# Moving tile pools of a hybrid attention/recurrence block: head weights beside the recurrence, and three staging tiles for w_out

## The chip, the cores and the metric

The kernel runs on one core of a Trainium2 chip. The metric is the device time of one execution in microseconds (us); before the change its median was 1280.75 over 3 runs (1280.01 to 1283.48). The engines are TensorE (PE: matmuls; PEld: its weight loads), VectorE (DVE), ScalarE (ACT), GpSimd (POOL) and SyncE (SP), which issues nearly all DMAs here, in order, from one queue.

## The reference

One layer works on 2048 latent tokens (a grid of 32 rows and 64 columns) and 256 context tokens of width 1024:

```python
h  = rms_norm(x, g) * (1 + scale) + shift          # hc likewise from ctx
q, k, v, z_a, u, z_l = split(h @ w_in)             # w_in: 1024 x 3072, six parts of 512
k_c, v_c, u_c = parts of hc @ w_in
attn = neighbourhood_attention(rope(norm(q)), norm(q), rope(norm(k)), v, norm(k_c), v_c, rpb)
uc, ucc = depthwise_conv(u), depthwise_conv(u_c)   # width 4
y = forward RG-LRU(ucc, uc) + backward RG-LRU(ucc, uc)
mix = concat([attn * silu(z_a), y * silu(z_l)]) @ w_out
out = x + gate * mix
```

The attention has 8 heads of 64 channels, the recurrence 8 blocks of 64. A recurrence step is `h = a*h + b`, with `a` and `b` made from two sigmoid gates of `u` through block weights `lru_wa`, `lru_wx` of 64 x 64, one set for each direction. `gate` comes from the conditioning vector through `w_mod`.

## The kernel before

**Number format.** A product of full precision is made of three fast ones: every operand is split into a high part and the remainder (`hh`, `hl` for the tokens, `wh`, `wl` for weights; all float16 in the projections, a rounded 32-bit format in the recurrence and the output). So a group of weights goes through `wload` (DMA into `wraw`), and `wsplit` (L315): DVE reduces the greatest magnitude (L319), `allmax` and `pow2` make a power of two of it (two tiny matmuls in a PSUM bank `mm`, and some small DVE operations), ACT makes `wh` (L324), DVE `wl` (L325).

**Phase 1** (`phase1`, L483). `mods` forms the conditioning vectors from `w_mod`, `prep` the normalised and transposed tokens (`hh`, `hl`: 64 KB per partition, kept on the right side of SBUF), `tables` writes bias tables to DRAM. Then, for four groups c of 128 recurrence channels: `u_proj(c)` projects and convolves `u` into a tile `uc` (pool `uc`, two tiles), through staging tiles `us`; `lru(c)` (L411) makes the gates' matmuls for both directions (weights `gw`, split into `gh` and `gl`), and per direction exponentials, square roots and scans of 2304 columns on DVE. The sums of both directions are made by POOL (L471) and stored as `d_y` (L472). Inside `lru(c)`, a function `fill(d)` emits the projection of two blocks of the attention's gate `z_a` of group c (`silu_z`, tile `sz`), and in its first call asks for the next group of these weights (`z_group`). `gate` (L575) makes the output's gate from more `w_mod` rows; its tiles are in a pool of its own on the right.

**Phase 2** (`phase2`, L920). For each of eight heads, `head_proj` makes q, k, v (192 columns, L602 to L604) and `attention` the banded softmax and its product. The recurrence's gate `z_l` is made in between (`lru_gate`). The second half of `w_out` (k = 4 to 7) is split in phase 2 (L1020, on DVE).

**Output** (`build`, L1085). The pools `out` and `ow` open when phase 2's right pools have closed. The gate row is spread over the partitions (`grow`, L1096), the first half of `w_out` (k = 0 to 3) is loaded into one staging tile `wo` (L1012), copied to its high part on ACT (L1015) and subtracted on POOL (L1016), beside the attention of head 7. `out_half` loads a tile of the mix (`m`, L1028, two buffers) and splits it into `mh` (ACT, L1030) and `ml` (DVE, L1031); `out_sum` (L1034) multiplies; the result times `grow` is added to a tile `xo` of `x` and stored.

**What sets the order.** The code is written against a tile framework which plans each engine's order of instructions itself, by the dependencies and the order in which the program emits them. A tile of a tag gets its buffer in program order: the next tile of a tag with n buffers waits for the one n places before it. The PSUM banks (`mm`, `sl`, `pt` two each, `sc`, `po` one) are such tags too. A pool that is opened on the bytes of pools that have closed is planned behind the last instruction of those; at run time each tile waits for the users of its own bytes. `issue_after` and `later` shift an emission in the plan.

**Places in SBUF.** On the right lie, from the outer edge inward, `h` (64 KB), `z` (two tiles of 2 KB: `us`, `sz`, and in phase 2 `ry`), `w2` (head weights: `wraw` 6 KB, two pairs `wh`, `wl` of 3 KB), `w3` (6 KB) and `stg` (18 KB: `ST0`, `ST1`, `STc` and others). On the left lie the constants, `hc`, `w1` (weights of the u and z_a groups: two raw tiles, three pairs `wh`, `wl`; 20 KB), `uc` (18 KB), then `p0` until the preparation is over and after it `lru` (78 KB: `A`, `X`, `I` twice each, `uh`, `ul`, `gh`, `gl`, `gw`). `lru` reaches into the bytes which `w2` and the gate's tiles have from the right, so `w2` is opened behind `lru` (L573), and its `wraw` lies on `ul`. In phase 2, `att`, `w3` and `stg` lie on bytes of `lru`, `uc` and `w1` as well. In the output, `ow` (`grow`, `wo`, two `m`) lies inward of `out`, on `ST0`, `ST1` and `STc`.

Of the kernel before, what the change touches and what calls it, by code (L numbers as in the profile page):

```python
# [45 lines left out]
BW = [384, 512, 384]  # L46

MA = 6
HLV = (3, 7)

MX = 400
# [7 lines left out]
class K:  # L59
# [232 lines left out]
    def w_tiles(self, tag, n):  # L292

        if tag == "z":
            return [self.wp["z"].tile([128, KC, 128], F16, tag=x, name=x, bufs=3) for x in ("wh", "wl")]
        if tag == "l":
            return [self.wp["l"].tile([128, KC, 128], F16, tag=x, name=x, bufs=1) for x in ("wh", "wl")]
        return [self.wp["h"].tile([128, KC, 192], F16, tag=x, name=x, bufs=2)[:, :, 0:n] for x in ("wh", "wl")]

    def wload(self, parts, tag):  # L300

        n = sum(w for _, w in parts)
        wp = self.wp["z" if tag == "z" else "h"]
        if tag == "z":
            raw = wp.tile([128, KC, n], F32, tag="raw", name="wraw", bufs=2)
        else:
            raw = wp.tile([128, KC, 192], F32, tag="raw", name="wraw", bufs=1)[:, :, 0:n]
        wv = self.a["w_in"].rearrange("(k p) n -> p k n", p=128)
        o = 0
        for c, w in parts:  # L310
            self.nc.sync.dma_start(raw[:, :, o:o + w], wv[:, :, c:c + w])
            o += w
        return raw, n, tag
# [97 lines left out]
    def lru(self, c, uc, p, fill):  # L411
# [4 lines left out]
        t = lambda x: p.tile([128, N], F32, tag=x, name=x, bufs=2)  # L416
        A, X = t("A"), t("X")
        gl = p.tile([128, 4, 128], F32R, tag="gl", name="gl", bufs=1)
        gw = p.tile([128, 4, 128], F32, tag="gw", name="gw", bufs=1)
        nc.gpsimd.memset(gw, 0.0)  # L420
        for g, nm in enumerate(("lru_wa", "lru_wx")):
            for f in range(2):
# [60 lines left out]
    def phase1(self, left, right):  # L483
# [14 lines left out]
        with ExitStack() as s1:  # L498
# [20 lines left out]
                return uc  # L519

            with ExitStack() as s0:
                p0 = self.pool(s0, "p0")
                mods = self.mods(p0)
                next(mods)
                with self.tc.issue_after(self.last.ins):
                    g0 = self.wgroup([(CU, 128)], "z", early=True)
                xs = next(mods)
                with self.tc.issue_after(self.last.ins):
                    self.prep(p0, 2, 1, hhc, hlc, xs, True)
                    ug[0] = u_group(0, g0)  # L530
                    ug[1] = u_group(1)
                    nxt = self.prep_in(p0, a["x"], 4, 0)
                    for tb in range(4):
                        xs = nxt
                        if tb < 3:
                            nxt = self.prep_in(p0, a["x"], 4, tb + 1)
                        self.prep(p0, 4, 0, self.hh[tb], self.hl[tb], xs)
                    with ExitStack() as s3:
                        self.tables(self.pool(s3, "tab", side="right"))
                    self.softplus(p0)  # L540
                    ucs = [u_proj(0), u_proj(1)]
                    with ExitStack() as s3, self.tc.issue_after(self.xld.ins), self.tc.issue_after(self.hh_op.ins):
                        self.gate(self.pool(s3, "gate", side="right"))
            za = []

            def z_group():
                c = len(za)
                g = self.wgroup([(CZA + 128 * c, 128)], "z", slow=c > 0)
                nc.vector.tensor_scalar(self.zs[:, c:c + 1], g[2], 0.5, None, ALU.mult)
                za.append(g)  # L550
            with ExitStack() as s2:
                p = self.pool(s2, "lru")
                ug[2] = u_group(2)
                z_group()

                def z_units(c, d):
                    wh, wl, _ = za[c]
                    for tb in (2 * d, 2 * d + 1):
                        z = self.silu_z(self.zp, self.bank("mm"), wh, wl, self.zs[:, c:c + 1], tb)
                        dz = self.d_z[c][tb].rearrange("p (j f x) -> p f j x", j=4, f=2)  # L560
                        for f in range(2):
                            zf = z[:, 256 * f:256 * f + 256]
                            nc.sync.dma_start(dz[:, f, 0:3], zf[:, 32:224].rearrange("p (j x) -> p j x", j=3))
                            nc.sync.dma_start(dz[:, f, 3].rearrange("p (e x) -> p e x", e=2),
                                              bass.AP(zf.tensor, zf.offset, [list(zf.ap[0]), [224, 2], [1, 32]]))
                    if d == 0 and c < 3:
                        z_group()

                for c in range(4):
                    self.lru(c, ucs[c], p, lambda d, c=c: z_units(c, d))  # L570
                    if c < 2:
                        ucs.append(u_proj(c + 2))
            self.wp["h"] = self.pool(self.wright, "w2", bufs=2, side="right")  # L573

    def gate(self, p):  # L575

# [429 lines left out]
    def out_weights(self, ks, room):  # L1006

        nc = self.nc
        wo = self.a["w_out"].rearrange("(k p) n -> k p n", p=128)
        for k in ks:  # L1010
            w = room()
            nc.sync.dma_start(w, wo[k])  # L1012
            W = self.hp.tile([128, 2, D], F32R, tag="h", name="W")
            if k < 4:
                nc.scalar.copy(W[:, 0], w)  # L1015
                nc.gpsimd.tensor_tensor(W[:, 1], w, W[:, 0].bitcast(F32), ALU.subtract)  # L1016
            else:
                s = self.zs[:, k:k + 1]
                nc.scalar.activation(W[:, 0], w, AF.Copy, scale=s)
                nc.vector.scalar_tensor_tensor(W[:, 1], w, s, W[:, 0].bitcast(F32), ALU.mult, ALU.subtract)  # L1020
            self.wo.append((k, W))
# [34 lines left out]
    def out_proj(self, p, q, tb, opened):  # L1056
        nc, a = self.nc, self.a
        for i in range(4 * tb, 4 * tb + 4):
            pos = opened.pop(i, None)
            M1 = self.out_half(p, q, i, 1) if pos is None else None  # L1060
            M = self.out_half(p, q, i, 0)
            x = p.tile([128, D], F32, tag="xo", name="xo", bufs=2)
            for r, src in self.tile_rows(a["x"], i):
                nc.sync.dma_start(x[r], src)
            for f in range(2):
# [19 lines left out]
def build(tc, a):  # L1085
    with ExitStack() as ctx:
        k = K(ctx, tc, a)
        k.setup()
        k.vectors()
        with ExitStack() as right, ExitStack() as left:  # L1090
            k.phase1(left, right)
            att = k.phase2(left, right)
            p = k.pool(right, "out", side="right")
            q = k.pool(right, "ow", side="right")
            k.grow = q.tile([128, D], F32, name="grow")
            tc.nc.sync.dma_start(k.grow, bass.AP(k.d_g.tensor, 0, [[0, 128], [1, D]]))  # L1096
            k.out_weights(range(4), lambda: q.tile([128, D], F32, tag="wg", name="wo", bufs=1))
            op = k.out_open(p, q, 0)
            next(op)
            next(att)  # L1100
            with k.later(100):
                opened = {0: next(op)}
            for tb in range(4):
                next(att, None)
                k.out_proj(p, q, tb, opened)
# [34 lines left out]
```

## Time and profile before

| | us |
|---|---|
| median of 3 runs | 1280.75 (1280.01 to 1283.48) |
| the profiled execution | 1277.88 |
| its span in the profile | 1276.1 |
| PE busy | 1122.0 |
| DVE busy | 926.6 |
| ACT busy | 615.2 |
| POOL busy | 478.7 |

The span runs from the first to the last profiled instruction; the execution's own time is 1.78 us longer. The mean granted TensorE clock of this execution is 0.936 of full speed. Busy shares are averages over stages with different limits; the timelines of the places that the change touches say more.

### The profile page before, as it was taken

How to read it: one execution, taken by the hardware profiler on the slowest of the kernel's cores; microseconds unless marked ns; L12 is line 12 of the kernel's file. 1: busy time of each engine (PE TensorE's matmuls, PEld its weight loads, DVE VectorE, ACT ScalarE, POOL GpSimd, SP SyncE). 2: the span in 40 equal slices, each digit the busy share in tenths (PEclk: the TensorE clock that was granted, in tenths of full speed). 3: DMA queues.
4: the chain of work that ended last, by engine and by line, in shares of the span. 5: the costliest groups of instructions: out<-in, count | busy, mean ns of one | idle time of the engine just before them, and what ended most of it. 6: DMA issues, size and time to landing. Idle time of an engine off the chain costs nothing. (4 is left out here: it accounts for less than half of the span.)

```text
span 1276.1 us, 26205 instructions
## 1 busy us (share of the span) xinstructions
PE 1122.0 (88%) x9964; PEld 858.8 (67%) x9964; DVE 926.6 (73%) x2546; ACT 615.2 (48%) x1189; POOL 478.7 (38%) x863
## 2 busy tenths in 40 slices
PE   7777889689981879999999999999999976999997
PEld 1434345445540767889878898788887755778786
DVE  7798655989775677888978989798887863544432
ACT  1597116876773225555655555555556452231210
POOL 0144002234122087566566556565564552000000
PEclk9788899699996889999999999999999997999999
DMA  9846980011024414344543435334354346346452
GB/s 349 284 153 237 312 250 26 4 50 54 17 67 99 93 34 85 83 97 96 118 88 83 95 86 137 82 89 76 86 129 103 89 99 177 95 134 176 122 149 83
DMA packets 196014, 149.50 MB, mean 117 GB/s; under 512 B 129453, under 2 KB 168109, under 8 KB 195887
## 3 DMA queue, kind: packets, MB, share of 16 engines
q1 hardware_dynamic: 195887, 147.82, 43.3%
q8 instruction: 78, 1.28, 0.4%
q14 instruction: 49, 0.40, 0.1%
HBM read 96.42 MB, written 47.94 MB: 113 GB/s over the span
## 5 line engine op out<-in xcount | busy, mean ns | idle before, releaser
L602 PE MATMUL mm<-wh,hh 128*128 128x192 f16 x960 | 236.9, 247 | 0.0
L603 PE MATMUL mm<-wl,hh 128*128 128x192 f16 x960 | 236.9, 247 | 0.0
L604 PE MATMUL mm<-wh,hl 128*128 128x192 f16 x960 | 236.9, 247 | 0.0
L893 DVE TENSOR_TENSOR Pl<-pt,Ph 128x384 f16<-128x384 f32 (+1 forms) x256 | 127.4, 516 | 56.2 <-ACT Ph L892 55.7
L344 PE MATMUL mm<-hh,wh 128*128 128x512 f16 x384 | 150.3, 392 | 12.9 <-DVE sz L480 7.6
L345 PE MATMUL mm<-hl,wh 128*128 128x512 f16 x384 | 149.2, 389 | 8.3 <-POOL hl L289 7.9
L885 ACT ACTIVATE SP<-SP,nb 128x640 f32<-128x640 f32 (+1 forms) x128 | 110.7, 881 | 91.9 <-DVE nb L883 87.7
L346 PE MATMUL mm<-hh,wl 128*128 128x512 f16 x384 | 149.0, 388 | 0.0
L892 ACT CAST Ph<-pt 128x384 f16<-128x384 f32 (+1 forms) x256 | 107.1, 453 | 67.5 <-PE pt L891 66.6
L891 PE MATMUL pt<-id,SP 128*128 128x128 f32 x704 | 115.6, 282 | 0.6 <-ACT SP L885 0.2
L602 PEld LDWEIGHTS <-hh 128*128 128x128 f16 x1024 | 100.6, 98 | 3.6 <-issue 2.8
L603 PEld LDWEIGHTS <-hh 128*128 128x128 f16 x1024 | 100.5, 98 | 1.8 <-issue 0.3
L604 PEld LDWEIGHTS <-hl 128*128 128x128 f16 x1024 | 100.5, 98 | 1.0
L880 DVE CUSTOM_DVE_ANT_0 SP<-sl,b,m 128x384 f32<-128x384 f32 (+1 forms) x128 | 93.2, 735 | 6.6 <-PE sl L828 4.5
L828 PE MATMUL sl<-qk,qt 128*128 128x128 f16 (+2 forms) x800 | 78.2, 230 | 16.9 <-DVE m L880 6.9
L898 PEld LDWEIGHTS <-Ph 128*128 128x128 f16 x1408 | 79.1, 97 | 9.9 <-ACT Ph L892 3.1
L891 PEld LDWEIGHTS pt<-id,SP 128*128 128x128 f32 x704 | 78.9, 143 | 5.2 <-ACT SP L885 1.2
L443 POOL TENSOR_TENSOR ul<-uc,uh 128x512 fp32r<-128x512 f32 (+1 forms) x20 | 33.0, 1679 | 123.3 <-ACT uh L442 123.3
L346 PEld LDWEIGHTS <-wl 128*128 128x128 f16 x416 | 41.6, 100 | 55.4 <-issue 16.9
L717 POOL TENSOR_TENSOR ST<-P,ST 128x256 f16<-128x256 f32 x64 | 43.4, 679 | 93.7 <-ACT ST L716 93.2
L898 PEld LDWEIGHTS <-Pl 128*128 128x128 f16 x704 | 65.8, 98 | 16.1 <-DVE Pl L893 9.8
L345 PEld LDWEIGHTS <-wh 128*128 128x128 f16 x416 | 41.9, 101 | 50.3 <-issue 14.0
(303 smaller groups left out, 3060.9 us busy)
## 6 DMA issues: line engine op xcount, KB each, us to landing
b<-d_e SPq DMA_DIRECT2D x32, 288.0 KB
wm<-w_mod SPq DMA_DIRECT2D x16, 512.0 KB
x<-x SPq DMA_DIRECT2D x16, 512.0 KB
wraw<-w_in SPq DMA_DIRECT2D x12, 512.0 KB
d_t<-te SPq DMA_DIRECT2D x12, 512.0 KB
d_e<-d_t SPq DMA_DIRECT2D x8, 768.0 KB
wraw<-w_in SPq DMA_DIRECT2D x24, 256.0 KB
b<-d_e SPq DMA_DIRECT2D x16, 384.0 KB
```

The source lines that it names most:

```text
L344: nc.tensor.matmul(out, wh[:, k, :], hh[:, k, :n], start=(k == 0), stop=False)
L345: nc.tensor.matmul(out, wh[:, k, :], hl[:, k, :n], start=False, stop=False)
L346: nc.tensor.matmul(out, wl[:, k, :], hh[:, k, :n], start=False, stop=(k == KC - 1))
L602: nc.tensor.matmul(out, hh[:, k, t0:t0 + 128], wh[:, k, :], start=(k == 0), stop=False)
L603: nc.tensor.matmul(out, hh[:, k, t0:t0 + 128], wl[:, k, :], start=False, stop=False)
L604: nc.tensor.matmul(out, hl[:, k, t0:t0 + 128], wh[:, k, :], start=False, stop=(k == KC - 1))
L880: nc.vector.tensor_tensor_reduce(SP[:, 0:W], sl[:, 0:W], bt[:, CT[j], 0:W], self.qs, m1, ALU.add, ALU.max, accum_out=m2)
L885: nc.scalar.activation(SP[:, :N], SP[:, :N], AF.Exp, bias=nb)
L891: nc.tensor.transpose(pt[:, i - c0, :], SP[:, 128 * i:128 * i + 128], self.id32)
L892: nc.scalar.copy(Ph[:, c0:c1], pt)
L893: nc.vector.tensor_tensor(Pl[:, c0:c1], pt, Ph[:, c0:c1], ALU.subtract)
L898: nc.tensor.matmul(pv[:, jj], P[:, i, :], v[:, w:w + 66], start=(i == j0 == 0), stop=(i == nch - 1 and j0 == 2))
```

## The change

- The head weights' pool `w2` opens before `lru` instead of after it. For room, `lru` and `w1` shrink: the pairs `wh`, `wl` of the u and z_a groups have two buffers instead of three (`WB`); the raw tiles of the first two u groups lie in `p0`, later ones in a single raw tile of `w1`; the recurrence's gate weights `gw` are loaded into a tile of the tag `z` (pool `zp`), whose two buffers they share in program order with `us` and `sz`. The order of that tag becomes: `us` of u-projections 0 and 1, `gw` 0, `sz` 0 (four), `us` 2 (four), `gw` 1, `sz` 1, `us` 3, `gw` 2, `sz` 2, `gw` 3, `sz` 3. After it, `lru` overlaps neither `w2` nor the gate's tiles.
- The subtraction of the even tiles k = 0 and 2 of `w_out` goes to DVE, that of k = 1 and 3 stays on POOL.
- The staging tile of k = 0 to 3 becomes the tag `xo` of the pool `out`, with three buffers (it had one of its own; `xo` had two). `ow` is opened before `out`, so that `grow` and the two tiles `m` now lie on `wh` and `wl` of `w2`, and the `xo` tiles on `ST0`, `ST1` and `STc`; `mh` stays where it was.

```diff
@@ -46,6 +46,7 @@
 BW = [384, 512, 384]
 
 MA = 6
+WB = 2
 HLV = (3, 7)
 
 MX = 400
@@ -292,7 +293,7 @@
     def w_tiles(self, tag, n):
 
         if tag == "z":
-            return [self.wp["z"].tile([128, KC, 128], F16, tag=x, name=x, bufs=3) for x in ("wh", "wl")]
+            return [self.wp["z"].tile([128, KC, 128], F16, tag=x, name=x, bufs=WB) for x in ("wh", "wl")]
         if tag == "l":
             return [self.wp["l"].tile([128, KC, 128], F16, tag=x, name=x, bufs=1) for x in ("wh", "wl")]
         return [self.wp["h"].tile([128, KC, 192], F16, tag=x, name=x, bufs=2)[:, :, 0:n] for x in ("wh", "wl")]
@@ -302,7 +303,7 @@
         n = sum(w for _, w in parts)
         wp = self.wp["z" if tag == "z" else "h"]
         if tag == "z":
-            raw = wp.tile([128, KC, n], F32, tag="raw", name="wraw", bufs=2)
+            raw = (self.p0 or wp).tile([128, KC, n], F32, tag="raw", name="wraw", bufs=2 if self.p0 else 1)
         else:
             raw = wp.tile([128, KC, 192], F32, tag="raw", name="wraw", bufs=1)[:, :, 0:n]
         wv = self.a["w_in"].rearrange("(k p) n -> p k n", p=128)
@@ -416,7 +417,7 @@
         t = lambda x: p.tile([128, N], F32, tag=x, name=x, bufs=2)
         A, X = t("A"), t("X")
         gl = p.tile([128, 4, 128], F32R, tag="gl", name="gl", bufs=1)
-        gw = p.tile([128, 4, 128], F32, tag="gw", name="gw", bufs=1)
+        gw = self.zp.tile([128, 512], F32, tag="z", name="gw", bufs=2).rearrange("p (g c) -> p g c", g=4)
         nc.gpsimd.memset(gw, 0.0)
         for g, nm in enumerate(("lru_wa", "lru_wx")):
             for f in range(2):
@@ -519,7 +520,7 @@
                 return uc
 
             with ExitStack() as s0:
-                p0 = self.pool(s0, "p0")
+                self.p0 = p0 = self.pool(s0, "p0")
                 mods = self.mods(p0)
                 next(mods)
                 with self.tc.issue_after(self.last.ins):
@@ -529,6 +530,7 @@
                     self.prep(p0, 2, 1, hhc, hlc, xs, True)
                     ug[0] = u_group(0, g0)
                     ug[1] = u_group(1)
+                    self.p0 = None
                     nxt = self.prep_in(p0, a["x"], 4, 0)
                     for tb in range(4):
                         xs = nxt
@@ -548,6 +550,7 @@
                 g = self.wgroup([(CZA + 128 * c, 128)], "z", slow=c > 0)
                 nc.vector.tensor_scalar(self.zs[:, c:c + 1], g[2], 0.5, None, ALU.mult)
                 za.append(g)
+            self.wp["h"] = self.pool(self.wright, "w2", bufs=2, side="right")
             with ExitStack() as s2:
                 p = self.pool(s2, "lru")
                 ug[2] = u_group(2)
@@ -570,7 +573,6 @@
                     self.lru(c, ucs[c], p, lambda d, c=c: z_units(c, d))
                     if c < 2:
                         ucs.append(u_proj(c + 2))
-            self.wp["h"] = self.pool(self.wright, "w2", bufs=2, side="right")
 
     def gate(self, p):
 
@@ -1013,7 +1015,8 @@
             W = self.hp.tile([128, 2, D], F32R, tag="h", name="W")
             if k < 4:
                 nc.scalar.copy(W[:, 0], w)
-                nc.gpsimd.tensor_tensor(W[:, 1], w, W[:, 0].bitcast(F32), ALU.subtract)
+                eng = nc.gpsimd if k % 2 else nc.vector
+                eng.tensor_tensor(W[:, 1], w, W[:, 0].bitcast(F32), ALU.subtract)
             else:
                 s = self.zs[:, k:k + 1]
                 nc.scalar.activation(W[:, 0], w, AF.Copy, scale=s)
@@ -1059,7 +1062,7 @@
             pos = opened.pop(i, None)
             M1 = self.out_half(p, q, i, 1) if pos is None else None
             M = self.out_half(p, q, i, 0)
-            x = p.tile([128, D], F32, tag="xo", name="xo", bufs=2)
+            x = p.tile([128, D], F32, tag="xo", name="xo", bufs=3)
             for r, src in self.tile_rows(a["x"], i):
                 nc.sync.dma_start(x[r], src)
             for f in range(2):
@@ -1090,11 +1093,11 @@
         with ExitStack() as right, ExitStack() as left:
             k.phase1(left, right)
             att = k.phase2(left, right)
+            q = k.pool(right, "ow", side="right")
             p = k.pool(right, "out", side="right")
-            q = k.pool(right, "ow", side="right")
             k.grow = q.tile([128, D], F32, name="grow")
             tc.nc.sync.dma_start(k.grow, bass.AP(k.d_g.tensor, 0, [[0, 128], [1, D]]))
-            k.out_weights(range(4), lambda: q.tile([128, D], F32, tag="wg", name="wo", bufs=1))
+            k.out_weights(range(4), lambda: p.tile([128, D], F32, tag="xo", name="wo", bufs=3))
             op = k.out_open(p, q, 0)
             next(op)
             next(att)
```

## Rows read from the trace of the kernel before

**Rows 1.** The page: each engine's busy time, share of the span and instructions.

```profile
PE 1122.0 (88%) x9964; PEld 858.8 (67%) x9964; DVE 926.6 (73%) x2546; ACT 615.2 (48%) x1189; POOL 478.7 (38%) x863
```

**Rows 2.** The windows view: window, its length, busy time by engine, PEclk, DMA share, GB/s.

```profile
0.00:31.90 31.90, 24.19 (x62) 5.86 (x63) 23.89 (x64) 4.58 (x8) 2.36 (x12) 0.95 0.95 349
196.00:401.70 205.70, 166.45 (x731) 94.23 (x730) 171.72 (x182) 147.50 (x187) 55.28 (x30) 0.89 0.14 36
382.80:414.70 31.90, 5.36 (x25) 2.23 (x23) 17.16 (x13) 12.28 (x13) 8.00 (x29) 0.65 0.40 99
1049.00:1092.00 43.00, 27.22 (x154) 20.22 (x154) 13.05 (x28) 13.26 (x22) 11.14 (x9) 0.76 0.56 153
```

**Rows 3.** The timeline of PE at the phase boundary (start, duration, instruction, wait).

```profile
387.78 0.38 PE L346 MATMUL mm<-hh,wl 128*128 128x512 f16 x1
...
420.14 0.26 PE L602 MATMUL sl<-wh,hhc 128*128 128x128 f16 x1 [2.42 <-ACT wh L324]
```

**Rows 4.** The timeline of DVE at the phase boundary.

```profile
390.61 0.68 DVE L480 SCALAR_TENSOR_TENSOR sz<-sz,mm 128x512 f32<-128x512 f32 x1
...
396.24 5.46 DVE L468 TENSOR_TENSOR_SCAN A<-A,X 128x256 f32<-128x256 f32 x3
414.38 1.75 DVE L319 TENSOR_REDUCE wm<-wraw 128x1 f32<-128x1536 f32 x1 [12.68 <-DMA wraw<-w_in]
...
420.12 1.82 DVE L325 SCALAR_TENSOR_TENSOR wl<-wraw,ws,wh 128x1536 f16<-128x1536 f32 x1 [0.81 <-ACT wh L324]
```

**Rows 5.** The timeline of SP, its DMA queue, at the phase boundary.

```profile
403.85 2.63 SPq L472 DMA_DIRECT2D d_y<-A  x2
...
407.05 3.29 SPq L311 DMA_DIRECT2D wraw<-w_in  x3
```

**Rows 6.** The timeline of ACT at the phase boundary.

```profile
418.51 1.57 ACT L324 ACTIVATE wh<-wraw,ws 128x1536 f16<-128x1536 f32 x1 [23.38 <-DVE ws L104]
```

**Rows 7.** The timeline of PE, first attention gate and start of the recurrence.

```profile
156.45 0.61 PE L344 MATMUL mm<-hh,wh 128*128 128x512 f16 x1 [4.70 <-ACT wh L324]
...
194.14 1.02 PE L594 MATMUL pt<-gacc,gone 128*1 128x512 f32 x2
...
206.96 0.47 PE L447 MATMUL sl<-uh,gh 128*128 128x256 f32 x1
...
225.71 0.58 PE L447 MATMUL sl<-uh,gh 128*128 128x256 f32 x1 [4.34 <-ACT uh L442]
```

**Rows 8.** The timeline of SP in the same stretch.

```profile
160.05 5.05 SPq L311 DMA_DIRECT2D wraw<-w_in  x2
...
197.10 1.34 SPq L423 DMA_DIRECT2D gw<-lru_wa  x2
```

**Rows 9.** The timeline of DVE, second gate's weights and the recurrence.

```profile
169.97 1.22 DVE L319 TENSOR_REDUCE wm<-wraw 128x1 f32<-128x1024 f32 x1 [0.35 <-DMA wraw<-w_in]
...
225.52 0.68 DVE L452 SCALAR_TENSOR_TENSOR I<-I,uc 128x512 f32<-128x512 f32 x1
...
248.40 0.54 DVE L364 TENSOR_SCALAR uc<-us,cw,vec 128x512 f32<-128x512 f32 x1
```

**Rows 10.** The timeline of PE where head 7 meets the output projection.

```profile
1062.89 0.79 PE L1040 MATMUL pt<-W,mh 128*128 128x512 f32 x1 [8.91 <-ACT mh L1030]
```

**Rows 11.** The chain of waits, 1050 to 1092 (start, duration, what).

```profile
1054.43 7.71 DMA m<-d_re
...
1066.07 6.10 DMA wo<-w_out
...
1073.32 2.41 POOL W L1016
```

**Rows 12.** One line's instructions, L1020: operation, count, ns min/median/max.

```profile
L1020 DVE SCALAR_TENSOR_TENSOR W<-wo,zs,W x4: 1283/1284/1483, 980.0 to 1004.0; 128x1024 fp32r<-128x1024 f32 x4
```

**Rows 13.** The timelines of POOL and DVE, the last but one pair of sums.

```profile
360.42 7.17 POOL L471 TENSOR_TENSOR A<-A 128x1024 f32<-128x1024 f32 x2 [8.40 <-issue]
...
362.59 6.16 DVE L452 SCALAR_TENSOR_TENSOR I<-I,uc 128x512 f32<-128x512 f32 x3
```

## The prediction

> **What bounds the kernel now.** I read the page's engine shares first [rows 1]: PE is busy 88% of the span and nothing else over 73%, so time is mostly PE time, and a change that leaves every matmul in place can only win where PE stands idle. The windows view says where that is [rows 2]. In the 31.90 us from 382.80, PE is busy 5.36 us; in the recurrence stretch 196.00 to 401.70 it is busy 166.45 of 205.70 us and DVE 171.72; in the 43 us from 1049, where head 7's attention and the output projection meet, PE is busy 27.22, so 15.8 us are idle there. These three places are where the change works.
>
> At the phase boundary PE's timeline [rows 3] shows the last matmul of the recurrence phase at 387.78 and the first of head 0 at 420.14: 32 us, broken only by the scale's tiny matmuls. DVE's timeline [rows 4] shows what ran meanwhile: the last scans, which start at 396.24 and end at 401.70, then nothing until the reduction of head 0's weights at 414.38, released by the load of `wraw`. SP's [rows 5] shows why that load is late: it is issued at 407.05, behind the `d_y` stores that POOL's last sums release, because `w2` lies on bytes of `lru` and opens behind it. Then comes a chain: reduction 1.75, its end (416.13) to `wh` 2.38, `wh` 1.57 on ACT [rows 6], `wl` 1.82 on DVE [rows 4], PE.
>
> **The change, part by part** (terms against the profiled execution: 1277.88 us, span 1276.1; it is 2.87 below the median of the runs, which I add back at the end).
>
> *A, head 0's weights ahead of the boundary.* `w2` now opens before `lru` and shares no byte with it, so the three loads no longer wait for `d_y`: the store wait, the 7.3 us from the issue at 407.05 to the reduction at 414.38, and the reduction leave the path. What is late next? The scale needs a bank of `mm`, granted in program order behind the last gate units; the first of the last two gives it back at 391.3 (390.61 + 0.68 [rows 4]). From there 2.4 + 1.6 + 1.8 gives 397.0 if DVE were free; behind the scans the end is 401.70 + 2.2 = 403.9 (rest of the scale and `wl`). Head 0's PE start moves from 420.14 to between 397 and 403.9: −16 to −23. I take −18, nearer the late end, since DVE's scans come first in its order. A tile of the head's first evacuation still lies on `lru`'s bytes, but PE fills its banks first, and `d_y` is issued at 403.85 [rows 5], so this is covered. If that cover goes, it is at most the 2.6 us of that issue.
>
> *B, the recurrence.* Three edits meet here. (1) `lru` no longer lies on the gate's tiles. Now the first recurrence starts on PE at 206.96, behind the gate's matmuls at 194.14 and its own weights, issued at 197.10 [rows 7, 8]; its banks still go to the gate's two matmuls first, so it can start at about 196: up to −11. (2) Two `wh`/`wl` pairs in place of three: the first attention gate's pair waits for the second u-projection, and its load queues behind the third u-group's. Its PE start of 156.45 [rows 7] then slides to where the second attention gate's is now: load issued 160.05 [rows 8], reduced from 169.97 [rows 9], the same chain of about 5.8 behind it: 175.7, so 19 us later for PE work of a kind that has slack, since DVE is the fuller engine there. It moves some 5 us of DVE splitting into the recurrence. (3) The recurrence's gate weights take a slot of `z`, in order behind the staging tiles of the next u-projection, so recurrence 1 may no longer start beside recurrence 0 at 225.71 [rows 7]. What fills DVE then is that same u-projection, which has to be done anyway.
> Counted as DVE's work alone, the end stays: 171.72 of 205.70 busy is 83%, and an earlier start with 5 us more work ends within 1 us of 401.70. Walked as a chain of dependencies with everything ready, the last scan would end near 377: −24, an estimate, 11 of it from the earlier start and 13 from waits inside. I take −6: half of the 11, since DVE nearly fills the stretch.
>
> *C, the output's weights.* PE's longest wait there, 8.91 us, ends at 1062.89 with `mh` [rows 10]. The chain shows `mh` waiting for `m`, issued at 1054.43 and 7.71 us on its way [rows 11], because `ow` lies on `ST`, which a transposing DMA of head 7 reads until just before. Now `m` and `grow` lie on `w2`'s dead tiles, so `m` can be there long before, and `mh`, whose place frees as the stretch begins, follows at once. Behind it each `wo` load waited for the one staging tile: 6.10 for a load, 1.15 from its landing to POOL's start (ACT's copy), 2.41 on POOL [rows 11], four times over. With three tiles, three loads go together; only the fourth waits, and only for the first subtraction. The same subtraction takes DVE 1.28 us in the four of the other half [rows 12], against POOL's 2.41; DVE is busy 13 of these 43 us, so its two fit in. Gain: between 0 (PE is fed by head 7's attention only, and the same idle reappears) and 13 (nearly all 15.8 idle; after 1092 PE is full to the end). I take −8, the 8.91 wait less about 1 for the cast. The third `xo` buffer I cost at nothing: behind 1092 PE never waits for it.
>
> *D, the start.* The third u-group's load is no longer held by its raw tile, so 512 KB may go out among the first loads, where the queue moves 349 GB/s [rows 2]: 0 to +1.5. I take +1.5.
>
> One row speaks against splitting the subtractions over two engines. In the recurrence, three operations of L452 took 6.16 us beside POOL's sums, where one alone takes 0.68 [rows 9, 13]: DVE stood still while POOL ran. [...]
>
> **Sum:** −18 − 6 − 8 + 1.5 = −30.5: 1247.4 for a profiled run, 1250.3 with the 2.87 of the median. I say 1250.
>
> **The rivals.**
> *Fast (0.20).* DVE's order in the recurrence had slack and the chain decides: end near 377. For it: PE and DVE both have idle time there [rows 2] and recurrence 0 waits for weights. Against: 83% is full for a chain that hops between three engines. B becomes −24: 1229.4, as a median 1232.
> *Recurrence given back (0.20).* The later gate units and splits end the scans 4 us later, A gives its lower end 16, and C only 2, since head 7's softmax rather than `mh` limits PE. −16 + 4 − 2 + 1.5 = −12.5: 1265.4, as a median 1268.
> *Slower: the weights' slot serialises the recurrences (0.10).* Its place is the `z` pool, two slots in program order. Recurrence 1's weights get the slot of the third staging tile of u-projection 2, whose first DVE pass is at 248.40 [rows 9]; with its taps (about 2.5) and the 9.9 from weight load to first matmul (197.10 to 206.96 [rows 7, 8]), recurrence 1 starts near 261 instead of 225.71. If nothing absorbs these 35 us, the end is 437, head 0 starts at 439 where it was 420.14: +18.6 − 8 + 1.5 = +12, 1290, as a median 1293. It decides from an end of the recurrence later than 424.4, 22.7 behind today's: there A has become +6.5 and is eaten by C and D. Against it: between 226 and 262 DVE has the rest of recurrence 0 and u-projection 2 to do.
> *It doesn't do what it says (0.05).* If SP's order still keeps the head's loads behind `d_y` (the queue is in order, and a load planned late stays late), A is 0, and with C of −3 the run is 1276, as a median 1279: no change that counts.
>
> **How the numbers follow.** The forecast (A near its middle, B small) has 0.45, and its own range is 1241 to 1262: B from 0 to −15, C from −13 to 0. What a measurement of this kernel can tell from no change is about 0.3%, 3.8 us. Faster than that: the forecast, the fast case and the given-back case, 0.85. The same: 0.05. Slower: 0.10. The range of 8 in 10 runs from just below the fast case to just above the given-back one: 1229 to 1271. It leaves out the last two cases and the fringes.
>
> **What would show it.** Right: `wraw` of head 0 loaded and reduced before 390; PE's gap behind the last gate unit ending near 397 to 402; the first matmul of recurrence 0 near 196 and the last scan near 396; the PE wait of 8.91 gone and PE busy over 34 of the 43 us from where head 7's attention ends. Wrong: the SP timeline with the head's loads still behind `d_y`; a last scan behind 402, with DVE waiting for matmuls of a recurrence whose weights came late; or PE's idle time in the out stage as long as before, with the name of another releaser. If head 0 starts earlier and the end does not move by as much, a later stage gave it back, and my sum is wrong in supposing that everything behind the boundary just shifts.

## The result and the profile after

| | before | after |
|---|---|---|
| median, us | 1280.74 (7 runs) | 1268.18 (7 runs, 1264.4 to 1270.9) |
| ratio of after to before | | 0.991 (95% interval 0.9886 to 0.9934) |
| span of the profiled execution | 1276.1 | 1266.4 |
| PE's first matmul of recurrences 0 to 3 | 207.0, 225.7, 283.3, 347.6 | 168.6, 256.4, 331.5, 372.8 |
| end of the last scan | 401.7 | 419.8 |
| PE's first matmul of head 0 | 420.1 | 411.5 |
| last start of a head projection's matmul (L602, after: L604) | 1026.3 | 1028.7 |
| from there to the end of the span | 249.8 | 237.7 |

The kernel became faster by 12.6 us, where 30.5 were forecast. (One run of before, at 1912.11, was disturbed; the ratio leaves it out.) The table splits the 9.7 us by which the spans differ: head 0 starts 8.6 earlier, the heads take 11.0 longer, and the rest is 12.1 shorter.

First the windows of [rows 2], of the changed kernel (window, its length, busy time of PE, PEld, DVE, ACT and POOL, granted clock, DMA share, GB/s). Line numbers are now one to three higher than before.

```profile
196.00:401.70 205.70, 175.86 (x804) 94.74 (x802) 158.96 (x180) 135.62 (x172) 43.74 (x24) 0.94 0.17 45
1049.00:1092.00 43.00, 37.22 (x241) 29.27 (x241) 23.38 (x56) 16.80 (x33) 7.28 (x8) 0.92 0.65 178
```

In the out stage, PE is busy 37.22 of 43 us where it was 27.22. In the recurrence's stretch DVE is busy 158.96 us where it was 171.72: by 401.70 it has less done, not more. PE's timeline, to be compared with [rows 3, 7], shows the four recurrences and head 0:

```profile
168.64 0.58 PE L448 MATMUL sl<-uh,gh 128*128 128x256 f32 x1 [20.12 <-DVE gh L427]
...
256.39 0.39 PE L448 MATMUL sl<-uh,gh 128*128 128x256 f32 x1 [1.88 <-DVE gh L427]
...
331.53 0.47 PE L448 MATMUL sl<-uh,gh 128*128 128x256 f32 x1
...
372.77 0.47 PE L448 MATMUL sl<-uh,gh 128*128 128x256 f32 x1
...
411.50 0.26 PE L604 MATMUL sl<-wh,hhc 128*128 128x128 f16 x1 [4.50 <-ACT wh L325]
```

Recurrence 0 starts 38 us earlier than before, but recurrence 1 starts 31 later, and its first matmul waits for `gh`, the high part of the weights `gw`. SP's timeline, to be compared with [rows 5, 8], gives the reason:

```profile
160.51 3.06 SPq L424 DMA_DIRECT2D gw<-lru_wx  x2
...
193.01 1.96 SPq L312 DMA_DIRECT2D wraw<-w_in  x3
...
251.56 1.25 SPq L424 DMA_DIRECT2D gw<-lru_wa  x2
...
323.93 1.26 SPq L424 DMA_DIRECT2D gw<-lru_wa  x2
...
421.99 2.65 SPq L473 DMA_DIRECT2D d_y<-A  x2
424.73 1.10 SPq L933 DMA_DIRECT2D rope<-rope  x1
```

The weights of recurrence 0 are loaded at about 160, those of recurrence 1 only at 251.56 and those of recurrence 2 at 323.93. The three loads at 193.01 are head 0's, far ahead of the boundary, where they were at 407.05. What stands last here is what is late now: `d_y` and the rope table, which was issued at 406.53 before. DVE's timeline shows the last operations ahead of the load of recurrence 1's weights, and then the boundary, to be compared with [rows 4]:

```profile
247.58 0.54 DVE L365 TENSOR_SCALAR uc<-us,cw,vec 128x512 f32<-128x512 f32 x1
...
248.29 2.32 DVE L370 SCALAR_TENSOR_TENSOR uc<-us,cw,uc 128x511 f32<-128x511 f32 x3
...
406.09 0.27 DVE L114 TENSOR_REDUCE av<-mm 1x1 f32<-1x128 f32 x1
...
407.49 0.14 DVE L117 COPY am<-mm 128x1 f32<-128x1 f32 x1
...
408.87 0.15 DVE L102 TENSOR_SCALAR p<-am 128x1 int32<-128x1 int32 x1
...
412.62 1.81 DVE L326 SCALAR_TENSOR_TENSOR wl<-wraw,ws,wh 128x1536 f16<-128x1536 f32 x1
...
417.46 2.35 DVE L469 TENSOR_TENSOR_SCAN A<-A,X 128x1024 f32<-128x1024 f32 x1
```

The third staging tile of u-projection 2 is read from 247.58, its last three taps from 248.29 for 2.32; at 250.61 its slot of `z` is free, POOL sets it to zero from 250.72 to 251.53, and at 251.56 `gw` is loaded into it. At the boundary the scale's small steps (406.09, 407.49, 408.87) and `wl` (412.62) now stand ahead of the last scans, which end at 419.81.

The matmuls of heads 0 to 7, grouped by line and operand, give the stretch of the heads in both kernels (operation, tiles, count, ns min/median/max, first and last start):

```profile
L602 PE MATMUL mm<-wh,hh x960: 242/246/364, 431.0 to 1026.3; 128*128 128x192 f16 x192
```

```profile
L604 PE MATMUL mm<-wh,hh x960: 242/246/368, 423.1 to 1028.7; 128*128 128x192 f16 x192
```

It begins 7.9 earlier (431.0 to 423.1) and ends 2.4 later. Where head 0's lead goes can be seen on DVE's timeline, before and after:

```profile
441.61 1.22 DVE L319 TENSOR_REDUCE wm<-wraw 128x1 f32<-128x1024 f32 x1 [0.89 <-DMA wraw<-w_in]
```

```profile
441.38 1.22 DVE L320 TENSOR_REDUCE wm<-wraw 128x1 f32<-128x1024 f32 x1 [7.95 <-DMA wraw<-w_in]
```

and on SP's, where the load of these weights is issued, before and after:

```profile
437.75 0.40 SPq L311 DMA_DIRECT2D wraw<-w_in  x1
```

```profile
432.77 0.79 SPq L312 DMA_DIRECT2D wraw<-w_in  x1
```

This is the reduction of the first weights of `z_l`, and in DVE's order it stands ahead of the scales of head 0's q and k. The load is issued at the end of a run of transfers that begins with `d_y` at 421.99, and it takes 8.6 us from issue to use, against 3.9 before; DVE is idle for 7.95 of them. POOL's first product of q and k starts at 445.78 where it was 446.81, so 1.0 is left of the 8.6. The out stage, on ACT's timeline, is as the forecast described it, to be compared with [rows 10, 11]:

```profile
1054.65 0.61 ACT L1033 CAST mh<-m 128x512 fp32r<-128x512 f32 x1
...
1062.31 1.05 ACT L1017 CAST W<-wo 128x1024 fp32r<-128x1024 f32 x1 [1.94 <-DMA wo<-w_out]
1064.36 1.05 ACT L1017 CAST W<-wo 128x1024 fp32r<-128x1024 f32 x1 [1.00 <-DMA wo<-w_out]
1066.40 1.05 ACT L1017 CAST W<-wo 128x1024 fp32r<-128x1024 f32 x1 [0.99 <-DMA wo<-w_out]
...
1069.36 1.05 ACT L1017 CAST W<-wo 128x1024 fp32r<-128x1024 f32 x1 [0.26 <-DMA wo<-w_out]
```

The mix tile is made into `mh` at 1054.65 where it was 1062.21, and the four `W` follow at 1062.31 to 1069.36 where the last was made at 1086.36.

### The profile page after: what moved, and what is told of

Its sections match the earlier page's. It is cut to its first block, busy times and chain, and to the rows that moved or that the text cites. A ratio compares the mean times of both kernels' runs of the same rounds, so it can differ in the third digit from the quotient of the medians.

```text
span 1266.4 us, 26204 instructions
## 1 busy us (share of the span) xinstructions
PE 1116.4 (88%) x9964; PEld 854.8 (67%) x9964; DVE 926.4 (73%) x2548; ACT 618.0 (49%) x1189; POOL 472.2 (37%) x861
## 5 line engine op out<-in xcount | busy, mean ns | idle before, releaser
L604 PE MATMUL mm<-wh,hh 128*128 128x192 f16 x960 | 237.0, 247 | 1.7 <-DVE V L762 1.6
L604 PEld LDWEIGHTS <-hh 128*128 128x128 f16 x1024 | 100.6, 98 | 8.9 <-issue 5.2
L444 POOL TENSOR_TENSOR ul<-uc,uh 128x512 fp32r<-128x512 f32 (+1 forms) x20 | 30.5, 1553 | 151.0 <-ACT uh L443 150.9
```

What stands on the lines that cost most here:

```text
L604: nc.tensor.matmul(out, hh[:, k, t0:t0 + 128], wh[:, k, :], start=(k == 0), stop=False)
```

## The experiments

Each of the twelve runs was timed together with the kernel before on the same chip. Ratios are to the kernel before; only these are compared across groups, since its median was 1278.8, 1275.4, 1274.8 and 1276.4 on the chips of the four groups.

| run | ratio | 95% interval | last scan ends | head 0 starts |
|---|---|---|---|---|
| after | 0.991 | 0.9886 to 0.9934 | 419.8 | 411.5 |
| e1_gw_own | 0.9817 | 0.9796 to 0.9839 | 404.9 | 406.8 |
| e2_before_gw_z | 1.017 | 1.0152 to 1.0189 | 418.8 | 437.5 |
| e3_out_old | 1.0019 | 0.9999 to 1.004 | 418.1 | 409.8 |
| e4_before_out_new | 0.9903 | 0.988 to 0.9926 | 398.0 | 418.9 |
| e5_sub_pool | 0.9934 | 0.9916 to 0.9952 | 417.9 | 409.6 |
| e6_order_only | 0.9968 | 0.9951 to 0.9985 | 415.9 | 407.6 |
| e7_u3_w2 | 0.9863 | 0.9844 to 0.9883 | 407.7 | 409.6 |
| e9_po | 0.985 | 0.9821 to 0.9878 | 402.6 | 404.3 |
| e12_before_pairs | 0.9923 | 0.9896 to 0.9951 | 403.1 | 405.0 |
| e10_head0_early | 0.9757 | 0.973 to 0.9785 | 405.0 | 396.6 |
| e11_u_early | 0.9811 | 0.9786 to 0.9836 | 401.6 | 403.5 |
| e13_both_early | 0.9778 | 0.9744 to 0.9813 | 406.7 | 395.5 |

The two right columns come from one profiled execution each. Kernels with the same first phase place the last scan up to 4 us apart (398.0 and 401.7 for the old one, 415.9 to 419.8 for the changed one), so smaller differences in these columns say nothing.

**The recurrence's weights.** Two runs, from both sides. e1_gw_own is the changed kernel with this:

```diff
-        gw = self.zp.tile([128, 512], F32, tag="z", name="gw", bufs=2).rearrange("p (g c) -> p g c", g=4)
+        gw = p.tile([128, 4, 128], F32, tag="gw", name="gw", bufs=1)
```

> The changed kernel with one edit undone: gw has a tile of its own in lru again (lru ends at byte 140,832, still under w2 at 141,280). Theory 1 (the shared z slots hold gw 1 and gw 2 behind the staging tiles of the next u-projection, and so the recurrences run one after the other: 168.6, 256.4, 331.5, 372.8 on PE): recurrence 1 starts near 200, the last scan ends between 380 and 396 where the changed kernel has 419.8, head 0 starts by 398, and the median falls from 1268 to between 1245 and 1256. Theory 2 (the late end comes from the two pairs wh, wl and the single raw tile, which make the groups of u and z_a late): the last scan still ends past 412 and the median stays within 4 of 1268.

The median was 1253.9 (ratio 0.9817). SP issues recurrence 1's weights at 172.16, on its timeline:

```profile
172.16 1.25 SPq L424 DMA_DIRECT2D gw<-lru_wa  x2
```

and PE starts recurrence 1 and head 0 at:

```profile
230.21 0.47 PE L448 MATMUL sl<-uh,gh 128*128 128x256 f32 x1
...
406.75 0.26 PE L604 MATMUL sl<-wh,hhc 128*128 128x128 f16 x1 [7.43 <-ACT wh L325]
```

Theory 1 holds for the time, which lies in its interval; the size of its steps was off. Recurrence 1 starts at 230, not 200, the last scan ends at 404.9 rather than by 396, and head 0 starts at 406.8 rather than by 398. So the interval was met in part by luck: of the 13.1 us by which the last matmul of the head projections starts earlier than in the changed kernel (1028.7 to 1015.7), 4.8 are there at head 0's start, and 8.3 come in the heads, where DVE now waits 1.15 for the first weights of `z_l` instead of 7.95. The edit's cost in the changed kernel is 0.991 − 0.9817, 0.9% or 12 us. e2_before_gw_z is the same edit the other way round, in the kernel before (`lru` shrinks there by the 2 KB of `gw`):

> The kernel before with this edit alone: gw in the tag z. Theory 1: recurrence 1 starts near 250 instead of 225.7 and the last scan ends 15 to 40 later than 401.7; head 0, whose weights still wait for the last store, starts as much later, and the median rises from 1281 to between 1295 and 1320. Theory 2: no change beyond 4.

1299.3, 1.7% above, or 22 us: the last scan ended 17 later, and head 0, whose weights still wait for the last store, 17 later. Recurrence 1 on PE's timeline:

```profile
261.31 0.39 PE L447 MATMUL sl<-uh,gh 128*128 128x256 f32 x1 [1.67 <-DVE gh L426]
```

It starts at 261.31 and waits for `gh`; theory 2 falls in both runs. The cost is greater here, probably because the head cannot overlap the late end: it starts 18.7 behind the last scan, where in the changed kernel it starts 8.3 ahead of it.

**The output.** e3_out_old undoes its three edits in the changed kernel, e4_before_out_new makes them in the kernel before:

```diff
-                eng = nc.gpsimd if k % 2 else nc.vector
-                eng.tensor_tensor(W[:, 1], w, W[:, 0].bitcast(F32), ALU.subtract)
+                nc.gpsimd.tensor_tensor(W[:, 1], w, W[:, 0].bitcast(F32), ALU.subtract)
...
-            x = p.tile([128, D], F32, tag="xo", name="xo", bufs=3)
+            x = p.tile([128, D], F32, tag="xo", name="xo", bufs=2)
...
+            p = k.pool(right, "out", side="right")
             q = k.pool(right, "ow", side="right")
-            p = k.pool(right, "out", side="right")
...
-            k.out_weights(range(4), lambda: p.tile([128, D], F32, tag="xo", name="wo", bufs=3))
+            k.out_weights(range(4), lambda: q.tile([128, D], F32, tag="wg", name="wo", bufs=1))
```

> The changed kernel with the output's edits undone (one staging tile in ow, out opened before ow, all four subtractions on POOL). If the 12 us by which the stretch from the last head projection to the end is shorter in the changed kernel come from these edits: the median rises from 1268 to 1278 to 1282, with the 8.9 us wait of PE for mh back. If they come from what stands before it (other order of head 7): at most 1272.

> The kernel before with the output's edits alone. If these are worth 10 to 13 by themselves: 1268 to 1271. If they need the rest of the change: 1276 or more.

1280.5 (1.0019) and 1265.2 (0.9903): the output's edits are worth 1.1% (14 us) in the one and 1.0% (12 us) in the other. What is left of the change without them is no gain at all. PE's wait for `mh` is back in e3_out_old:

```profile
1062.36 0.80 PE L1042 MATMUL pt<-W,mh 128*128 128x512 f32 x1 [7.95 <-ACT mh L1032]
```

e5_sub_pool undoes the split over the engines alone, with the edit below; e6_order_only has that edit too and one staging tile in `ow` again, so that of the output's edits only the opening order stays:

```diff
-                eng = nc.gpsimd if k % 2 else nc.vector
-                eng.tensor_tensor(W[:, 1], w, W[:, 0].bitcast(F32), ALU.subtract)
+                nc.gpsimd.tensor_tensor(W[:, 1], w, W[:, 0].bitcast(F32), ALU.subtract)
```

> The changed kernel with all four subtractions of w_out's first half on POOL again. If the split over two engines has a part in the output's gain (2 of 4 subtractions shorter by 1.1, and no queue on POOL): the median rises by 2 to 4 from 1268. If the early mix tile and the three staging tiles give all of it: within 2 of 1268.

> The changed kernel with ow still opened before out, but one staging tile (in ow) and all subtractions on POOL. If the mix tile's early load gives the gain (PE's wait of 8.9): the median is 1269 to 1273. If the staging gives it, because each W is late by a load: 1276 to 1281.

0.9934 and 0.9968. So the order alone gives 1.0019 − 0.9968 = 0.5% (6.5 us, intervals apart). It makes the mix tile early, and in e6_order_only the first two loads of `wo` as well, because `wo` then lies in `ow` on the same dead tiles:

```profile
1033.16 0.42 SPq L1014 DMA_DIRECT2D wo<-w_out  x1
...
1041.94 0.53 SPq L1014 DMA_DIRECT2D wo<-w_out  x1
```

In e3_out_old these are issued at 1054.38 and 1065.81. How much of the 0.5% belongs to each is not shown. The three staging tiles in their place add 0.3% (4 us; the intervals just touch). The split over two engines adds 0.2% (3 us), and since the intervals of e5_sub_pool and of the changed kernel overlap, that part is not shown.

**The weights' buffers.** e12_before_pairs is the kernel before with the two pairs and the one raw tile alone (`WB` = 2, and `p0` kept for the first two raw tiles, as in the change), in which `w2` still opens behind `lru`:

```diff
-            return [self.wp["z"].tile([128, KC, 128], F16, tag=x, name=x, bufs=3) for x in ("wh", "wl")]
+            return [self.wp["z"].tile([128, KC, 128], F16, tag=x, name=x, bufs=WB) for x in ("wh", "wl")]
...
-            raw = wp.tile([128, KC, n], F32, tag="raw", name="wraw", bufs=2)
+            raw = (self.p0 or wp).tile([128, KC, n], F32, tag="raw", name="wraw", bufs=2 if self.p0 else 1)
```

> The kernel before with the weights' buffers of the change alone: two pairs wh, wl and one raw tile in w1 (the first two raw tiles in p0), so that lru moves off the gate's tiles; gw keeps its tile, w2 still opens behind lru, the output is the old one. By e1_gw_own, in which the recurrence starts 36 us earlier but ends at 404.9 where the kernel before has 401.7, these edits give nothing by themselves: last scan between 400 and 407, head 0 some 18 behind it, median within 6 of the kernel before's, more likely above it. By the prediction's term (6 us earlier): last scan near 396, median 4 to 8 below the kernel before.

Neither expectation held: 0.9923, 10 us faster. The last scan ended at 403.1, as expected, but head 0 started at 405.0, 2 behind it instead of 18. SP's timeline says why:

```profile
192.18 0.24 SPq L598 DMA_DIRECT2D d_g<-grow  x1
192.52 1.86 SPq L312 DMA_DIRECT2D wraw<-w_in  x3
```

Head 0's three loads are issued at 192.52, right behind the gate's store, with the pool opened where it always was. What held them before was not the place of the opening in the program but the bytes: once `lru` ends below `w2`, they wait for nothing but the gate. Moving the opening gives nothing that can be seen: from e12_before_pairs to e1_gw_own, which has that move and the output's edits, is 0.9923 − 0.9817 = 1.1%, as much as the output's edits alone.

**What is late in e1_gw_own.** The next runs look for the 9 us between 396, the latest end expected, and the 404.9 measured, and for what is late at the boundary. e7_u3_w2 gives u-projection 3 weights in `w2`, free of the two pairs:

```diff
-                wh, wl, osc = g or self.wgroup([(CU + 128 * c, 128)], "z", slow=c > 1)
+                wh, wl, osc = g or self.wgroup([(CU + 128 * c, 128)], "h" if c == 3 else "z", slow=c > 1)
```

> e1_gw_own with one more edit: the weights of the u-projection 3 use a raw tile and a wh, wl pair of w2, which is idle then, so they no longer wait for the second of the two pairs of w1. Theory: what still holds the recurrence in e1_gw_own is that pair (recurrence 3 starts its main part at 354, right behind the last convolution pass of u-projection 3 at 352). Then recurrence 3 starts by 340, the last scan ends 8 to 15 earlier than 404.9, head 0 as much, and the median falls from 1254 to 1240 to 1248. Rival: DVE's share of work in the stretch sets the end, and u-projection 3 merely takes its turn; the end moves by less than 4 and the median stays within 4 of 1254.

0.9863: not faster than e1_gw_own but 0.5% slower (6 us), more than the rival allowed; why was not traced. The pair is not what holds u-projection 3, and the theory falls. e11_u_early adds to it an earlier place in the program:

```diff
                 def z_units(c, d):
                     wh, wl, _ = za[c]
+                    if d and c < 2:
+                        ucs.append(u_proj(c + 2))
...
-                    if c < 2:
-                        ucs.append(u_proj(c + 2))
```

> e7_u3_w2 (u-projection 3's weights in w2) with each u-projection emitted ahead of the last two gate units and the last scans of the recurrence before it. Theory: the end of the recurrence is set by the order in which DVE is given its work (in e1_gw_own DVE is 97% busy from 290 to 350 and 40% from 350 to 380, when recurrence 3 waits for u-projection 3); with u-projection 3 earlier, recurrence 3 starts by 340, the last scan ends at 385 to 397 where e7_u3_w2 has 407.7, and the median falls to 1243 to 1252. Rival: the tile uc, which recurrence 1 reads to its end, holds it back: the last scan stays past 403 and the median within 4 of e7_u3_w2.

0.9811, 0.5% below e7_u3_w2, with the last scan at 401.6, so between theory and rival; but e1_gw_own, without either edit, has 0.9817. The order matters against e7_u3_w2, and the end near 402 stays. What holds it there was not settled. The windows of e1_gw_own show where to look:

```profile
290.00:320.00 30.00, 23.73 (x104) 14.94 (x103) 29.09 (x42) 24.80 (x31) 5.58 (x2) 0.84 0.20 64
320.00:350.00 30.00, 26.82 (x107) 11.53 (x106) 29.57 (x25) 8.76 (x14) 9.03 (x5) 0.84 0.09 36
350.00:380.00 30.00, 29.31 (x138) 15.69 (x136) 12.07 (x17) 18.83 (x23) 2.50 (x2) 1.00 0.22 45
```

DVE is full from 290 to 350 and busy 12.07 of 30 us from 350 to 380. There PE is the full engine, 29.31 of 30 us: 107 of its 138 matmuls are those of gate units, and DVE's longest waits, 4.27 and 4.74 us, are for their `sz`. Recurrence 3's work on DVE is done behind them, to 404.9. Whether it would end earlier with the gate units behind its matmuls was not tried.

At the boundary, e9_po makes head 0's scale in another PSUM bank:

```diff
-        self.mb = "mm"
         p = self.pool(left, "att")
...
                     self.hw[i] = self.wsplit(*self.head_w(i))
+                self.mb = "mm"
```

> e1_gw_own with another edit: the scale of heads 0 and 1 is made in the bank po, as in phase 1, rather than in mm, which the last gate units hold. Theory: the bank is what is late at the boundary (the scale's reduction in PSUM ran at 398.6, between the last gate units and the scans), so with another bank the scale, wh and wl are ready before the scans, head 0 starts on PE before 400 where e1_gw_own has 406.75, and the median falls by 4 to 7. Rival: head 0's first matmuls come earlier but what follows (q, k after them) waits for tiles on the bytes of lru, and the second head's start at 448 and the median stay within 2.

0.985, no gain, and head 0 still starts 1.7 behind the last scan (404.3 to 402.6), as in e1_gw_own (406.8 to 404.9). The bank is not it. DVE's timeline of e1_gw_own shows the thing itself:

```profile
400.01 0.12 DVE L117 COPY am<-mm 128x1 f32<-128x1 f32 x1
400.11 2.35 DVE L469 TENSOR_TENSOR_SCAN A<-A,X 128x1024 f32<-128x1024 f32 x1
402.38 0.13 DVE L102 TENSOR_SCALAR p<-am 128x1 int32<-128x1 int32 x1
402.50 2.35 DVE L469 TENSOR_TENSOR_SCAN A<-A,X 128x1024 f32<-128x1024 f32 x1
404.77 0.13 DVE L104 TENSOR_SCALAR p<-p 128x1 int32<-128x1 int32 x1
```

Each of the scale's dependent steps of 0.13 us stands behind a scan of 2.35 in the order planned for DVE. So e10_head0_early emits head 0's split ahead of recurrence 3:

```diff
                 for c in range(4):
+                    if c == 3:
+                        self.hw = {0: self.wsplit(*self.head_w(0))}
                     self.lru(c, ucs[c], p, lambda d, c=c: z_units(c, d))
...
-            self.hw, self.bias, self.o = {}, [], {}
+            self.bias, self.o = [], {}
...
-                for i in range(2):
-                    self.hw[i] = self.wsplit(*self.head_w(i))
+                self.hw[1] = self.wsplit(*self.head_w(1))
```

> e1_gw_own with the split of head 0's weights emitted ahead of recurrence 3, so that the planner puts its small operations ahead of the last scans. Theory: at the boundary of e1_gw_own PE waits for the scale, whose dependent steps stand between the scans in DVE's order (400.0, 402.4, 404.8, wh at 405.1); then with wh and wl made long before, head 0 starts behind the last gate unit, before 398, and the median falls by 4 to 9. Rival: head 0's first matmuls start earlier, but its q and k wait for tiles on the bytes of lru, so that head 1 starts within 2 of 447.97 and the median stays within 3.

0.9757, 1246.1 us, 0.6% under e1_gw_own, inside the theory's range. `wl` is made at 353.94 on DVE, and on PE head 0 follows the last gate unit without a gap:

```profile
353.94 1.81 DVE L326 SCALAR_TENSOR_TENSOR wl<-wraw,ws,wh 128x1536 f16<-128x1536 f32 x1
```

```profile
396.35 0.38 PE L347 MATMUL mm<-hh,wl 128*128 128x512 f16 x1
396.57 0.22 PE L606 MATMUL sl<-wh,hhc 128*128 128x128 f16 x1
```

Of the 10.2 by which head 0 starts earlier than in e1_gw_own, 8.1 are left at the last matmul of the head projections (1007.5 to 1015.7). e13_both_early joins e10_head0_early and e11_u_early:

> e11_u_early and e10_head0_early together: gw in its own tile, u-projection 3's weights in w2, u-projections ahead of the last gate units, head 0's weights split ahead of recurrence 3. If the two gains (e10_head0_early 0.6% under e1_gw_own, e11_u_early 0.5% under e7_u3_w2) are of different stretches and add up: last scan near 400, head 0 before 393, a ratio of 0.970 to 0.975 to the kernel before. If head 0's early start already used the idle time of PE that an earlier end of the recurrence would shorten: 0.975 to 0.980, no better than e10_head0_early.

0.9778, no better than e10_head0_early: the two gains do not add. e10_head0_early has the lowest ratio found, 2.4% below the kernel before (its interval and that of e13_both_early overlap).

## Why the prediction was wrong

The direction was right, and the forecast was out by 18 us. That the rival "recurrence given back" named 1268 is luck: it had the scans ending 4 later, A at 16 and C at 2, where the scans ended 18 later, head 0 started 8.6 earlier and the output gave 12 to 14.

**B was the step that failed:** "What fills DVE then is that same u-projection, which has to be done anyway." The prediction saw the order of the `z` slots and even worked out when recurrence 1 would start (near 261; it was 256.4), as the mechanism of its rival on the slower side, and then argued it away with the work that DVE has meanwhile. The u-projection did stand there, but with one recurrence at a time and the steps of each hopping between PE, ACT and DVE, DVE had gaps: 158.96 us busy in the stretch where it was 171.72 before and is 170.90 in e1_gw_own, without the shared slot. Its waits there are 13.3 us for `I` and 11.2 for `X` from ACT (9.6 and 12.4 before), and 8.1 for weights still on their way, of which there were none before. The last scan came 18.1 later instead of 6 earlier. The rival's 35 held for the start of recurrence 1 in the kernel before (e2_before_gw_z, 225.71 to 261.31), but about half was absorbed: the last scan came 17 later and the whole 22. In the changed kernel 31 at recurrence 1 became 18 at the last scan, though recurrence 0 starts 38 earlier there and only 10 in e2_before_gw_z.

The part of B that stood on recurrence 0's early start was mis-sized too: in e1_gw_own and in e12_before_pairs, without the shared slot, the last scan ends at 404.9 and 403.1, not 395.7, though recurrence 0 starts 36 and 40 earlier. So nothing of an early start reached the end.

**A was right in its mechanism.** The loads went out at 193.01, and without the shared slot head 0 starts 1.9 behind the last scan (e1_gw_own) instead of 18.4: 16.5, where I took 18. The start itself, 406.8, lies behind my latest, 403.9: the scans end 3 later, and the steps of the scale stand between them. (My chain also put `wl` ahead of head 0's first matmul, which in [rows 3] waits for `wh` alone.) But I put it down to the opening of `w2` as well as to its bytes; e12_before_pairs shows that the bytes alone do it, and that the smaller `lru` and the earlier head are one step. Of the 15.1 by which head 0 starts earlier there, 10 are left in the time. In the changed kernel head 0 even starts 8.3 ahead of the last scan. That could not be kept: A's assumption that everything behind the boundary just shifts failed. `d_y` and the rope table now go out later than before (424.73 where it was 406.53), the first weights of `z_l` come behind them, DVE waits 7.95 for these ahead of head 0's q and k, and the heads take 11.0 longer, against 2.8 longer in e1_gw_own. Of the 11.0, 7.6 are lost by the time POOL starts its first product of q and k; the other 3.4 come later in the heads and were not traced.

**C was right in its mechanism and too small:** 12 to 14 where I took 8, at the upper end of my bounds of 0 and 13. The order alone, which removes the 8.91 wait I counted and makes the first two loads of `wo` early, gives 6.5; the staging, to which I gave nothing on top, is worth some 4 more. My 6.10 for a load, "four times over", was one row: the next two loads of that chain took 3.57 and 3.47. A price of two subtractions side by side could hardly show, since DVE's second one ran beside POOL's for 0.40 us alone: it took 1.48 us against 1.23 for the first, which had no POOL beside it.

**D was nothing that can be seen:** a third load of weights did go out among the first ones (one at 10.27, two at 19.29), and the first projection matmul came at 45.4 where it was 47.1; but e4_before_out_new, with the old first phase, has 45.1, so this is no gain either.

Added in ratios: buffers −0.77%, output −1.09%, the shared slot +0.93%: −0.93% together, where the whole measured −0.90% (interval 0.9886 to 0.9934).

## What to carry to other kernels

A tile that is small and short-lived is not free in a tag it shares: it inherits the program order of everything in that tag, and a load that must be early should never queue behind buffers that are freed late. When an early stage ends later while the next one starts earlier, look for the transfers and sums that still belong to the first, and for the loads that come behind them: here one such load took back most of head 0's lead. When a load is late because of where its bytes lie, moving the bytes is what helps; and when its small dependent steps are late, look at what stands between them in the engine's order.

## What the runs showed of the hardware

A DVE operation of one column took 2.19 us while POOL added two sums of 1024 columns, and 0.22 without it. From the changed kernel, DVE's timeline and POOL's:

```profile
241.07 2.19 DVE L370 SCALAR_TENSOR_TENSOR uc<-cy,cw,uc 128x1 f32<-128x1 f32 x1
...
248.16 0.22 DVE L370 SCALAR_TENSOR_TENSOR uc<-cy,cw,uc 128x1 f32<-128x1 f32 x1
```

```profile
237.17 8.37 POOL L472 TENSOR_TENSOR A<-A 128x1024 f32<-128x1024 f32 x2 [10.23 <-DVE A L469]
```

In [rows 13] such stretching is seen on operations of 512 columns: three took 6.16 us, where one alone took 0.68 [rows 9]. In e1_gw_own it stands on head 0's path, again from DVE's timeline and POOL's:

```profile
407.12 2.18 DVE L751 TENSOR_TENSOR vcf<-wo,zs 128x1 f32<-128x1 f32 x1
```

```profile
402.69 6.60 POOL L472 TENSOR_TENSOR A<-A 128x1024 f32<-128x1024 f32 x2 [47.09 <-issue]
```

The DVE operation ends at 409.30, POOL's sums at 409.29; `wl` follows on DVE, and PE waits 4.17 us for it behind its first matmul of head 0. In the kernel before, the same operation ran without POOL beside it (418.85) and took 0.14. What holds the DVE operation beside POOL was not shown.

Three loads of 512 KB of `w_out`, issued together at 1058.29, let ACT copy at 1062.31, 1064.36 and 1066.40: some 2.0 us apart. In the kernel before, where each waited for the one staging tile, they took 6.10 [rows 11] and, further down that chain:

```profile
1075.75 3.57 DMA wo<-w_out
...
1082.87 3.47 DMA wo<-w_out
```
